# An encoder block on one Trainium2 core: the second use of a weight tile loads the split parts that the first use stored

## The chip, the core and the metric

The kernel runs on one core of a Trainium2 chip. The core has a matrix engine (TensorE, PE in the profile), a vector engine (VectorE, DVE), a scalar engine (ScalarE, ACT), a general engine (GpSimd, POOL) and a queue engine (SyncE, SP), from which this kernel issues its DMA transfers. 16 DMA engines move data between the chip's memory and the on-chip buffers. The metric is the device time of one execution in microseconds.

## What is computed

One layer of an encoder, batch 1, 2048 tokens, width 1024, everything in float32:

```python
h  = rmsnorm(x, norm1_g)
P  = h @ w_in          # columns: attention q | k | v | SSD z | SSD x,B,C | SSD dt
yB = windowed_attention(q, k, v, sink, cos, sin)    # |i-j| <= 128, partial rotary
yA = ssd_mixer(z, xbc, dt, ...)                     # conv(5), SiLU, two chunked scans, gated norm
x  = x + concat(rmsnorm(yB), yA) @ w_out
x  = x + conv_glu_ffn(rmsnorm(x))                   # w_up, conv(3), gate, w_down
return rmsnorm(x, final_norm_g)
```

The change concerns the product `h @ w_in` alone, and of `w_in` the 1664 columns that come out with channels on the partitions: 13 tiles of 128 channels, `w_ch`, each 128 x 1024 floats (512 KB). The remaining columns (`w_t`) come out with tokens on the partitions and have loads of their own.

## The kernel before

**Three products for one.** PE multiplies in a rounded 32-bit format (fp32r). To keep float32's precision, each operand is split into a rounded high part and a low part that holds what the rounding left. `mm3` issues three matmuls for each product: high by high, high by low, low by high (L106, L107, L108). A weight tile therefore has to exist as two tiles, `whi` and `wlo`.

**The weight path.** All weight tiles stand in one list, `wplan`, in the order of their use, and `next_w` hands them out. `w_raw` loads a raw tile into the buffer tag `wraw` (L127). `w_split` casts it on ACT into `whi` (L141) and subtracts on DVE or POOL into `wlo` (L142):

```python
A.copy(hi[:, :m], raw[:, :m])
(V if i < WV or i in WVS else G).tensor_tensor(lo[:, :m], raw[:, :m], hi[:, :m].bitcast(F32), ALU.subtract)
```

The tables `WV` and `WVS` say by number in the list which tiles DVE subtracts. Each of the three tags has two buffers. `next_w` splits tiles i and i+1 and loads i+1 and i+2, so a tile is split while PE works on the one before it; its `whi` buffer comes free when PE is done with the tile two places before.

**Two halves.** The tokens are taken in two halves of 1024, each as two banks of 512. So each `w_ch` tile is used twice, and loaded and split twice (tiles 11 and 12 in the second half twice: once for each of its banks). A string for each half (`PLAN`) sets the order of the source: `F` is the pair of tiles 0 and 1, `C5` a tile of the convolved SSD input, `R10` a rotary tile of the attention, `t11` token-major tiles, letters steps of scan and attention. In the first half the list's numbers 0 to 12 are the tiles 0, 1, 5, 7, 4, 3, 2, 11, 10, 12, 6, 9, 8. In the second half numbers 13 to 25 are 0, 1, 2, 5, 4, 3, 6, 7, 10, 9, 8, 11, 12; numbers 26 to 37 are pieces of `w_out`, and 38 and 39 are tiles 11 and 12 again. From 40 on come `w_up`, `w_down` and the rest of `w_out`. Below, "tile 15" means number 15 of this list.

**What sets the order.** The kernel is written as a sequence of tile operations; a scheduler with a timeline simulation then fixes the order of instructions on every engine, ahead of the run. Every DMA of the kernel goes through SP's queue, in that order: a transfer that waits for a buffer holds up what stands behind it. Among these are the x tiles of the first normalisation (L244), the transposed x (L273), the rotary tables `cs` (L425; 512 KB each), the copies of the rotated rows (L433, L434), and the stores and loads of the scan and the attention.

**Consumers of the tables.** A rotary tile multiplies its table with the row factors on DVE (L428), then the PE result with the table (L436); the other terms run on POOL (L446, L447). L436 also reads the PSUM bank that PE then reuses.

Of the kernel before, what the change touches and what calls it, by code (L numbers as in the profile page):

```python
# [10 lines left out]
F32 = mybir.dt.float32  # L11
F32R = mybir.dt.float32r
# [5 lines left out]
P = 128  # L18
# [39 lines left out]
def block_kernel(ctx: ExitStack, tc: tile.TileContext, a: dict, out: bass.AP):  # L58
    nc = tc.nc
# [3 lines left out]
    wpool = ctx.enter_context(tc.tile_pool(name="wpool", bufs=2))  # L63
# [26 lines left out]
    def dram(name, shape):  # L90
        return dpool.tile(shape, F32, tag=name, name=name)
# [9 lines left out]
    s_d = dram("s_d", [6, P, 512])  # L101
    acs_d = dram("acs_d", [NC * H, 2, P])
    mix_d = dram("mix_d", [4, P, TB])

    def mm3(ps, whi, wlo, xhi, xlo, first, last):
        nc.tensor.matmul(ps, whi, xhi, start=first, stop=False)  # L106
        nc.tensor.matmul(ps, whi, xlo, start=False, stop=False)  # L107
        nc.tensor.matmul(ps, wlo, xhi, start=False, stop=last)  # L108
# [6 lines left out]
    wplan = [(a["w_ch"][c], 1024) for c in range(2)]  # L115
    wraws, wdone, wplace = {}, {}, {}
    wpos = [0]

    def w_raw(i):
        if i >= len(wplan) or i in wraws:  # L120
            return
        src, m = wplan[i]
        raw = wpool.tile([P, 1024], F32, tag="wraw", name="wraw")
        dst = raw[:, :m]
        if len(src.shape) == 3:
            dst = dst.rearrange("p (i n) -> p i n", i=2)
        nc.sync.dma_start(dst, src)  # L127
        wraws[i] = raw

    def w_split(i):  # L130
        if i >= len(wplan) or i in wdone:
            return
        w_raw(i)
        m = wplan[i][1]
        raw = wraws[i]
        if i in wplace:
            hi, lo = wplace.pop(i)
        else:
            hi = wpool.tile([P, 1024], F32R, tag="whi", name="whi")
            lo = wpool.tile([P, 1024], F32R, tag="wlo", name="wlo")  # L140
        A.copy(hi[:, :m], raw[:, :m])  # L141
        (V if i < WV or i in WVS else G).tensor_tensor(lo[:, :m], raw[:, :m], hi[:, :m].bitcast(F32), ALU.subtract)  # L142
        wdone[i] = (hi, lo)

    def next_w():
        i = wpos[0]
        wpos[0] += 1
        w_split(i)
        w_raw(i + 1)
        w_split(i + 1)  # L150
        w_raw(i + 2)
        return wdone.pop(i)
# [1048 lines left out]
    def wo_pair(cp, s):  # L1201
        src = a["w_out"][2 * cp : 2 * cp + 2, :, 512 * s : 512 * s + 512]
        return src.rearrange("c p n -> p c n"), 1024

    for half in range(2):
        for tok in PLAN[half].split():
            if tok == "F":
                wplan += [(a["w_ch"][c], 1024) for c in range(2 * half)]
            elif tok == "P3":
                wplan += [(a["w_ch"][c], 1024) for c in (11, 12)]  # L1210
            elif tok[0] in "HQ":
                wplan.append(wo_pair(int(tok[1]), "HQ".index(tok[0])))
            elif tok[0] in "CR":
                wplan.append((a["w_ch"][int(tok[1:])], 1024))
    wplan += [wo_pair(cp, 1) for cp in range(4)]
    wplan += [(a["w_ch"][c], 1024) for c in (11, 12)]
    for j in range(NB):
        for g, (k0, nk) in enumerate(GROUPS):
            wplan += [(a["w_up"][k0 + i, q], 1024) for i in range(nk) for q in range(2)]
# [146 lines left out]
    for j in range(NB):  # L1366
# [4 lines left out]
        for g, (k0, nk) in enumerate(GROUPS):  # L1371
# [3 lines left out]
            i = 0  # L1375
            if j == 0 and g == 0 and UP2:
# [9 lines left out]
                i = 2  # L1386
# [91 lines left out]
def build(arrays):  # L1478
    import concourse.bacc as bacc

    nc = bacc.Bacc("TRN2", target_bir_lowering=False, num_devices=1)
    aps = {
        n: nc.dram_tensor(f"in_{n}", v.shape, mybir.dt.from_np(v.dtype), kind="ExternalInput").ap()
        for n, v in arrays.items()
    }
    out = nc.dram_tensor("out_0", (D, S), F32, kind="ExternalOutput").ap()
    with tile.TileContext(nc, schedule_with_timeline_sim=True) as tc:
        block_kernel(tc, aps, out)
    return nc
# [9 lines left out]
```

## Time and profile before

| | before |
|---|---|
| median of 3 runs | 2496.29 us (2495.41 to 2500.74) |
| profiled execution | 2505.61 us |
| its span | 2503.8 us |
| PE busy | 2373.5 us, 95% |
| DVE, ACT, POOL busy | 70%, 43%, 45% |
| granted TensorE clock, mean | 0.975 of full speed |
| DMA | 332.13 MB, mean 133 GB/s |

A time in a row is counted from the start of the span of the profiled execution. In a window's row each engine has its busy time and its number of instructions; PEclk is the granted TensorE clock as a share of full speed, DMA the busy share of the 16 DMA engines. In a timeline row the bracket at the end holds the idle time just before the instruction and what ended it. In a row of waits stand the engine, its operation and line, what it waited for, then the total, the number of waits and the longest one.

### The profile page before, as it was taken

To read this page: it belongs to the slowest core of one execution; us is meant where nothing else is said; L and a number is where in the kernel's file an instruction comes from. 1 tells how busy PE (TensorE), PEld (TensorE's weight loads), DVE (VectorE), ACT (ScalarE), POOL (GpSimd) and SP (SyncE) were. 2 spreads that over 40 slices of the span, in tenths; PEclk is the share of its full clock that TensorE was granted. 3 is DMA by queue.
4 is the path that set the end of the run, shared out by engine and by line. 5 is a ranking of instruction groups with operands and counts; after the bars stand their busy time and mean duration, and the time that the engine had idled before them with its cause. 6 is when DMAs were issued, how large, how long until landed. Compare 5 with 4: busy or idle time off the path is not lost.

```text
span 2503.8 us, 31565 instructions
## 1 busy us (share of the span) xinstructions
PE 2373.5 (95%) x11440; PEld 1975.7 (79%) x11440; DVE 1761.6 (70%) x3116; ACT 1088.3 (43%) x1814; POOL 1126.9 (45%) x625
## 2 busy tenths in 40 slices
PE   8998999887899999999999999999999999999997
PEld 6877798766688887777788777777888877788887
DVE  5778778878786775468978685689686555844445
ACT  5444565444354444335444443254444433433334
POOL 1045314564545435445444443554444445544444
PEclk9999999998899999999999999999999999999998
DMA  6567445774433343333434333343443232332232
GB/s 225 178 198 224 126 147 186 247 246 149 141 116 122 127 140 97 101 112 122 126 131 137 99 133 114 90 129 119 129 127 96 84 114 89 118 101 93 93 94 84
DMA packets 176047, 332.13 MB, mean 133 GB/s; under 512 B 13202, under 2 KB 84242, under 8 KB 175892
## 3 DMA queue, kind: packets, MB, share of 16 engines
q1 hardware_dynamic: 175892, 330.12, 41.2%
q8 instruction: 90, 1.47, 0.2%
q14 instruction: 65, 0.53, 0.1%
HBM read 284.06 MB, written 44.71 MB: 131 GB/s over the span
## 4 chain that ended last, share of the span: by engine, by line
PE 50%; DVE 9%; POOL 2%; issue 2%; ACT 1%; DMA 1%; DVEq 0%; POOLq 0%; SPq 0%; ACTq 0%
PE up_b L108 9%; PE up_b L107 9%; PE up_b L106 9%; PE dn_b L106 3%; PE dn_b L107 3%; PE dn_b L108 3%; DVE fa L1047 2%; POOL wlo L142 2%; PE dn L107 2%; PE dn L106 2%; PE dn L108 2%; PE wo_b L108 2%; PE wo_b L106 2%; PE wo_b L107 2%; DVE m_lo L972 1%
## 5 line engine op out<-in xcount | busy, mean ns | idle before, releaser
L142 POOL TENSOR_TENSOR wlo<-wraw,whi 128x1024 fp32r<-128x1024 f32 (+1 forms) x306 | 739.0, 2416 | 901.8 <-ACT whi L141 849.8
L108 PE MATMUL up_b<-h_hi,wlo 128*128 128x512 f32 x1392 | 555.3, 399 | 15.9 <-POOL wlo L142 15.8
L107 PE MATMUL up_b<-h_lo,whi 128*128 128x512 f32 x1392 | 553.0, 398 | 4.7 <-DVE h_lo L208 4.7
L106 PE MATMUL up_b<-h_hi,whi 128*128 128x512 f32 x1392 | 554.3, 399 | 1.4 <-ACT whi L141 0.9
L141 ACT CAST whi<-wraw 128x1024 fp32r<-128x1024 f32 (+1 forms) x330 | 338.9, 1027 | 453.0 <-PE up_b L107 117.8
L1047 DVE SCALAR_TENSOR_TENSOR fa<-up_b,fcw,fa 128x511 f32<-128x511 f32 (+2 forms) x396 | 271.4, 686 | 206.1 <-ACT fa L1049 201.7
L108 PEld LDWEIGHTS up_b<-h_hi,wlo 128*128 128x128 f32 x1392 | 264.6, 190 | 79.8 <-POOL wlo L142 21.8
L107 PEld LDWEIGHTS up_b<-h_lo,whi 128*128 128x128 f32 x1392 | 264.3, 190 | 63.3 <-DVE h_lo L208 5.9
L106 PEld LDWEIGHTS up_b<-h_hi,whi 128*128 128x128 f32 x1392 | 264.1, 190 | 60.1 <-ACT whi L141 2.3
L106 PE MATMUL dn_b<-f,whi 128*128 128x512 f32 x528 | 211.4, 400 | 0.4 <-DVE x L1090 0.2
L107 PE MATMUL dn_b<-f,whi 128*128 128x512 f32 x528 | 208.8, 395 | 0.0
L108 PE MATMUL dn_b<-f,wlo 128*128 128x512 f32 x528 | 204.3, 397 | 0.0
L1069 ACT ACTIVATE fth<-fa 128x512 f32<-128x512 f32 (+1 forms) x88 | 55.6, 632 | 217.3 <-DVE fa L1047 165.3
L1074 ACT CAST f<-fth 128x512 fp32r<-128x512 f32 (+1 forms) x88 | 54.4, 620 | 207.6 <-DVE fth L1071 169.2
L1090 DVE TENSOR_TENSOR x<-x,dn_b 128x512 f32<-128x512 f32 x144 | 97.5, 680 | 61.0 <-PE dn_b L108 60.9
L1049 ACT ACTIVATE fa<-up_b,fcw 128x512 f32<-128x512 f32 x176 | 136.0, 774 | 0.2
L106 PEld LDWEIGHTS dn_b<-f,whi 128*128 128x128 f32 x528 | 99.7, 189 | 22.8 <-DVE x L1090 1.1
L108 PEld LDWEIGHTS dn_b<-f,wlo 128*128 128x128 f32 x528 | 99.3, 188 | 22.4 <-POOL wlo L142 0.3
L107 PEld LDWEIGHTS dn_b<-f,whi 128*128 128x128 f32 x528 | 99.2, 188 | 21.2
L875 DVE SCALAR_TENSOR_TENSOR ab<-ab,ldt,mask 128x128 f32<-128x128 f32 x256 | 106.7, 482 | 11.7 <-DMA ab<-acs_d 11.5
L1075 DVE TENSOR_TENSOR f<-fth,f 128x512 fp32r<-128x512 f32 (+1 forms) x88 | 79.2, 900 | 30.3 <-ACT f L1074 29.4
L106 PE MATMUL pj_b<-h_hi,whi 128*128 128x512 f32 x208 | 85.4, 411 | 12.3 <-ACT h_hi L235 7.1
(328 smaller groups left out, 5047.1 us busy)
## 6 DMA issues: line engine op xcount, KB each, us to landing
wraw<-in_w_up SPq DMA_DIRECT2D x176, 512.0 KB
wraw<-in_w_dn SPq DMA_DIRECT2D x64, 512.0 KB
wraw<-in_w_out SPq DMA_DIRECT2D x36, 512.0 KB
ab<-acs_d SPq DMA_DIRECT2D x32, 512.0 KB
wraw<-in_w_ch SPq DMA_DIRECT2D x28, 512.0 KB
wraw<-in_w_dn SPq DMA_DIRECT2D x32, 384.0 KB
ak<-ks_d SPq DMA_DIRECT2D x14, 768.0 KB
cs<-in_rope SPq DMA_DIRECT2D x20, 512.0 KB
```

Source lines behind the costliest of these rows:

```text
L106: nc.tensor.matmul(ps, whi, xhi, start=first, stop=False)
L107: nc.tensor.matmul(ps, whi, xlo, start=False, stop=False)
L108: nc.tensor.matmul(ps, wlo, xhi, start=False, stop=last)
L141: A.copy(hi[:, :m], raw[:, :m])
L142: (V if i < WV or i in WVS else G).tensor_tensor(lo[:, :m], raw[:, :m], hi[:, :m].bitcast(F32), ALU.subtract)
L875: (G if i < SUBP[0 if first else 1] else V).scalar_tensor_tensor(ab[:, i, d], ab[:, i, d], ldt[:, d, c, h : h + 1], mask3[:, 2 * d * P : ( ...
L1047: V.scalar_tensor_tensor(o, src, w(q), o, ALU.mult, ALU.add)
L1049: A.activation(ai[:, 0:TB], u, AF.Identity, bias=w(3), scale=w(2))
L1069: A.activation(th[:, :n], acc[:, 0, :n], AF.Tanh)
L1074: A.copy(fs[:, idx, 0, :n], th[:, :n])
L1075: V.tensor_tensor(fs[:, idx, 1, :n], th[:, :n], fs[:, idx, 0, :n].bitcast(F32), ALU.subtract)
L1090: V.tensor_tensor(xv, xv, ps[i], ALU.add)
```

## The change

In the first half, after a `w_ch` tile has been split, both parts are also stored to a new array `wch_d` in the chip's memory (L152 of the changed kernel). When the same tile comes up again, `w_split` takes two buffers and loads the two parts into them (L142 of the changed kernel); there is no raw load, no cast and no subtract. `w_ch` notes for each tile whether this is its first use. Thus 13 tiles make 26 stores of 512 KB; numbers 13 to 25, 38 and 39 make 30 loads of 512 KB, in place of 15 raw loads, 15 casts on ACT, and 15 subtracts (numbers 13, 14, 19, 21 and 25 on DVE, the other ten on POOL). The rest of the kernel is written as before.

```diff
+    wch_d = dram("wch_d", [13, 2, P, 1024])
+    wkeep, wch_at = {}, {}
...
+    def w_pair(i):
+        return [wpool.tile([P, 1024], F32R, tag=t, name=t) for t in ("whi", "wlo")]
+
     def w_raw(i):
-        if i >= len(wplan) or i in wraws:
+        if i >= len(wplan) or i in wraws or i in wsame:
             return
...
     def w_split(i):
         if i >= len(wplan) or i in wdone:
             return
+        if i in wsame:
+            wdone[i] = w_pair(i)
+            for t, src in zip(wdone[i], wsame[i]):
+                nc.sync.dma_start(t.bitcast(F32), src)
+            return
         w_raw(i)
...
         A.copy(hi[:, :m], raw[:, :m])
         (V if i < WV or i in WVS else G).tensor_tensor(lo[:, :m], raw[:, :m], hi[:, :m].bitcast(F32), ALU.subtract)
+        if i in wkeep:
+            for t, dst in zip((hi, lo), wkeep[i]):
+                nc.sync.dma_start(dst, t[:, :m].bitcast(F32))
         wdone[i] = (hi, lo)
...
+    def w_ch(c):
+        i = len(wplan)
+        dst = [wch_d[c, q] for q in range(2)]
+        if c in wch_at:
+            wsame[i] = dst
+        else:
+            wch_at[c] = i
+            wkeep[i] = dst
+        wplan.append((a["w_ch"][c], 1024))
```

The scheduler's order changes with it, in the input projection alone; three places follow. In the names below the number at the end only tells one buffer's use from another's. The first place is SP's queue near the start: `xt0` is an x tile, `wraw` the raw loads of tiles 2 and 3, `cs11` a rotary table, `xb3` transposed x. Before:

```order
L244 DMA xt0_170<-in_x 128x1024
L127 DMA wraw_231<-in_w_ch 128x1024
L127 DMA wraw_237<-in_w_ch 128x1024
L425 DMA cs11_512_1073<-in_rope 128x2x512
L273 DMA xb3_0_1552<-in_xT 128x512
```

Now:

```order
L254 DMA xt0_171<-in_x 128x1024
L152 DMA wch_d_109<-whi_224 128x1024
L152 DMA wch_d_109<-wlo_225 128x1024
L152 DMA wch_d_109<-whi_230 128x1024
L152 DMA wch_d_109<-wlo_231 128x1024
L133 DMA wraw_236<-in_w_ch 128x1024
L133 DMA wraw_244<-in_w_ch 128x1024
```

The four stores of tiles 0 and 1 have come between the x tile and the raw loads; the x tiles 1 to 3 stand some rows behind, in both.

The second place is SP's queue near the end of the first half, at the last rotary tile: `cs8` are its two tables, `rw` the copies of rotated rows, `qs_d` stored queries, `ct0` an operand of the scan. Before:

```order
L434 DMA rw8_512_1728<-rw8_512_1728 8x512
L454 DMA qs_d_103<-rw9_512_1638 128x2x512
L425 DMA cs8_512_1725<-in_rope 128x2x512
L433 DMA rw8_512_1728<-rw8_512_1728 8x512
L434 DMA rw8_512_1728<-rw8_512_1728 8x512
L454 DMA qs_d_103<-rw9_0_1650 128x2x512
L425 DMA cs8_0_1743<-in_rope 128x2x512
```

Now:

```order
L443 DMA rw8_512_1751<-rw8_512_1751 8x512
L444 DMA rw8_512_1751<-rw8_512_1751 8x512
L142 DMA whi_2144<-wch_d_109 128x1024
L142 DMA wlo_2145<-wch_d_109 128x1024
L435 DMA cs8_0_1766<-in_rope 128x2x512
L856 DMA ct0_4010<-ct_d0_94 128x2x128
L685 DMA pb_d_105<-stateb_3458 128x512
L464 DMA qs_d_103<-rw9_512_1663 128x2x512
L435 DMA cs8_512_1748<-in_rope 128x2x512
```

The two loads of tile 14 (`whi_2144`, `wlo_2145`) now stand ahead of both tables; its raw load stood farther up, before the copies of the rotated rows.

The third place is PE at the passage from the pair of tiles 13 and 14 (`pj0_1`, `pj1_1`, worked on in turn) to tile 15 (`pj2_1`) in the second half; `sc` are score products of the attention. Before, the last products of tile 13 are these, and after them 18 matmuls of `pj1_1` and four `sc` stand ahead of the first of tile 15:

```order
L108 MATMUL pj1_1_b0_2119<-h2_True_hi_2074,wlo_2122 128x512
L107 MATMUL pj0_1_b0_2117<-h2_True_lo_2075,whi_1671 128x512
L108 MATMUL pj0_1_b0_2117<-h2_True_hi_2074,wlo_1672 128x512
L106 MATMUL pj1_1_b0_2119<-h2_True_hi_2074,whi_2121 128x512
L107 MATMUL pj1_1_b0_2119<-h2_True_lo_2075,whi_2121 128x512
```

Now:

```order
L109 MATMUL pj0_1_b0_2140<-h2_True_lo_2098,whi_1696 128x512
L110 MATMUL pj0_1_b0_2140<-h2_True_hi_2097,wlo_1697 128x512
L110 MATMUL pj1_1_b0_2142<-h2_True_hi_2097,wlo_2145 128x512
L108 MATMUL pj1_1_b0_2142<-h2_True_hi_2097,whi_2144 128x512
L109 MATMUL pj1_1_b0_2142<-h2_True_lo_2098,whi_2144 128x512
L110 MATMUL pj1_1_b0_2142<-h2_True_hi_2097,wlo_2145 128x512
```

Tile 13's last two products have moved eight rows toward tile 15, so that ten matmuls of `pj1_1` and the four `sc` are left between.

## Rows read from the trace of the kernel before

**Rows 1.** The page: busy time of the engines; shares of the chain by engine.

```profile
PE 2373.5 (95%) x11440; PEld 1975.7 (79%) x11440; DVE 1761.6 (70%) x3116; ACT 1088.3 (43%) x1814; POOL 1126.9 (45%) x625
...
PE 50%; DVE 9%; POOL 2%; issue 2%; ACT 1%; DMA 1%; DVEq 0%; POOLq 0%; SPq 0%; ACTq 0%
```

**Rows 2.** PE's waits in 420 to 640: us in total, times, longest.

```profile
PE mt L936 <- ACT y L933: 6.4, 2, 4.5
PE pt L763 <- DVE mxs L737: 5.9, 1, 5.9
...
PE wh_b L107 <- DVE m_lo L972: 4.9, 5, 2.7
...
PE pq_b L108 <- POOL wlo L142: 0.5, 1, 0.5
```

**Rows 3.** Windows: length, PE, PEld, DVE, ACT, POOL, PEclk, DMA share, GB/s.

```profile
0.00:660.00 660.00, 587.59 (x2961) 500.20 (x2962) 505.48 (x809) 330.53 (x603) 261.85 (x188) 0.95 0.59 190
...
350.00:400.00 50.00, 50.00 (x290) 44.96 (x289) 35.98 (x94) 26.46 (x51) 9.83 (x7) 1.00 0.39 122
...
420.00:640.00 220.00, 182.91 (x942) 156.30 (x941) 181.65 (x316) 97.78 (x200) 120.87 (x93) 0.91 0.65 209
```

**Rows 4.** Groups of 0 to 660: count, busy us, mean ns, idle before and releasers.

```profile
L142 POOL TENSOR_TENSOR wlo<-wraw,whi 128x1024 fp32r<-128x1024 f32 x18 | 46.1, 2560 | 88.6 <-ACT whi L141 64.1 <-DVE x L997 12.4 <-DVE rsm L751 12.2
...
L141 ACT CAST whi<-wraw 128x1024 fp32r<-128x1024 f32 x42 | 43.9, 1045 | 44.9 <-PE pj_b L107 25.8 <-PE pq_b L107 7.1 <-DMA wraw<-in_w_out 4.0
...
L142 DVE TENSOR_TENSOR wlo<-wraw,whi 128x1024 fp32r<-128x1024 f32 x24 | 32.6, 1357 | 22.3 <-ACT whi L141 22.3
```

**Rows 5.** A window near the start, columns as in rows 3.

```profile
24.00:26.00 2.00, 2.00 (x10) 1.63 (x9) 0.40 (x2) 1.82 (x4) 0.00 (x0) 1.00 1.05 396
```

**Rows 6.** Timeline near the start, SP, ACT, DVE, PE: start, us, instruction.

```profile
1.20 0.42 SPq L127 DMA_DIRECT2D wraw<-in_w_ch  x1
...
22.37 1.58 SPq L127 DMA_DIRECT2D wraw<-in_w_ch  x2
27.74 2.40 SPq L244 DMA_DIRECT2D xt<-in_x  x3
...
5.13 1.04 ACT L141 CAST whi<-wraw 128x1024 fp32r<-128x1024 f32 x1 [3.11 <-DMA wraw<-in_w_ch]
...
30.48 1.04 ACT L141 CAST whi<-wraw 128x1024 fp32r<-128x1024 f32 x1
...
31.55 1.23 DVE L142 TENSOR_TENSOR wlo<-wraw,whi 128x1024 fp32r<-128x1024 f32 x1 [5.12 <-ACT whi L141]
...
34.70 0.40 PE L106 MATMUL pj_b<-h_hi,whi 128*128 128x512 f32 x1
```

**Rows 7.** Timeline and windows at the end of the rotary section, 210 to 228.

```profile
211.19 2.16 POOL L447 TENSOR_TENSOR cs<-cs,rw 128x512 f32<-128x512 f32 x1
...
212.11 2.31 DVE L428 TENSOR_TENSOR cs<-cs,rx_half 128x1024 f32<-128x1024 f32 x1
...
225.35 1.22 DVE L428 TENSOR_TENSOR cs<-cs,rx_half 128x1024 f32<-128x1024 f32 x1 [3.21 <-DMA cs<-in_rope]
...
227.35 0.64 PE L500 MATMUL tp_b<-thi,h_hi 128*128 128x328 f32 x1 [6.36 <-DVE cs L436]
...
210.00:215.00 5.00, 5.00 (x30) 4.51 (x29) 5.00 (x4) 1.28 (x3) 3.76 (x3) 1.00 0.38 128
...
224.00:227.30 3.30, 0.00 (x0) 0.00 (x0) 1.92 (x3) 0.00 (x0) 0.65 (x1) 0.50 1.04 330
...
227.40:230.60 3.20, 3.20 (x12) 3.20 (x13) 2.64 (x3) 1.61 (x4) 1.80 (x2) 0.50 0.77 234
```

**Rows 8.** Timeline at the passage to tile 15, ACT and PE.

```profile
275.37 1.05 ACT L141 CAST whi<-wraw 128x1024 fp32r<-128x1024 f32 x1 [4.98 <-PE pj_b L107]
...
280.04 0.40 PE L106 MATMUL pj_b<-h_True_hi,whi 128*128 128x512 f32 x1
```

**Rows 9.** Timeline of subtracts after 400 us, POOL and DVE.

```profile
405.23 2.44 POOL L142 TENSOR_TENSOR wlo<-wraw,whi 128x1024 fp32r<-128x1024 f32 x1 [4.68 <-ACT whi L141]
...
633.99 2.40 POOL L142 TENSOR_TENSOR wlo<-wraw,whi 128x1024 fp32r<-128x1024 f32 x1 [2.14 <-ACT whi L141]
...
518.49 2.25 DVE L142 TENSOR_TENSOR wlo<-wraw,whi 128x1024 fp32r<-128x1024 f32 x1 [0.77 <-ACT whi L141]
```

More of the change, by code (lines that the diff above doesn't have):

```diff
@@ L117, in block_kernel @@
     wpos = [0]
+    wsame = {}
+    def w_pair(i):
+        return [wpool.tile([P, 1024], F32R, tag=t, name=t) for t in ("whi", "wlo")]
     def w_raw(i):
-        if i >= len(wplan) or i in wraws:
+        if i >= len(wplan) or i in wraws or i in wsame:
             return
@@ L135, in w_split @@
         raw = wraws[i]
[L136 to L140, printed above, removed]
+        hi, lo = wplace.pop(i) if i in wplace else w_pair(i)
         A.copy(hi[:, :m], raw[:, :m])
         (V if i < WV or i in WVS else G).tensor_tensor(lo[:, :m], raw[:, :m], hi[:, :m].bitcast(F32), ALU.subtract)
+        if i in wkeep:
+            for t, dst in zip((hi, lo), wkeep[i]):
+                nc.sync.dma_start(dst, t[:, :m].bitcast(F32))
         wdone[i] = (hi, lo)
@@ L1203, in wo_pair @@
         return src.rearrange("c p n -> p c n"), 1024
+    def w_ch(c):
[7 more added lines that the diff above has]
+        wplan.append((a["w_ch"][c], 1024))
+    for c in range(2):
+        wch_at[c] = c
+        wkeep[c] = [wch_d[c, q] for q in range(2)]
     for half in range(2):
@@ L1207, in block_kernel @@
             if tok == "F":
-                wplan += [(a["w_ch"][c], 1024) for c in range(2 * half)]
+                for c in range(2 * half):
+                    w_ch(c)
             elif tok == "P3":
-                wplan += [(a["w_ch"][c], 1024) for c in (11, 12)]
+                w_ch(11)
+                w_ch(12)
             elif tok[0] in "HQ":
@@ L1213, in block_kernel @@
             elif tok[0] in "CR":
-                wplan.append((a["w_ch"][int(tok[1:])], 1024))
+                w_ch(int(tok[1:]))
     wplan += [wo_pair(cp, 1) for cp in range(4)]
-    wplan += [(a["w_ch"][c], 1024) for c in (11, 12)]
+    for c in (11, 12):
+        w_ch(c)
     for j in range(NB):
```

## The prediction

> **What bounds the kernel now.** I read the page first. TensorE (PE) is busy 95% of the span, and the page's chain that ended last is half PE and 9% VectorE (DVE) [rows 1]. Those shares add up to some 65% of the span: the chain leaves part of it uncovered, and it names mostly lines of the feed-forward part, which the change does not touch. What the change touches lies in the input projection, the first 660 us, so I read that stretch from windows and waits.
>
> The second thing to see is that PE is nearly always busy there too: 587.6 of 660 us, with 72 us idle, of which 37 us lie in 420 to 640 [rows 3]. So everything that the change could give back is bounded by those idle times, and by the clock that falls after some of them. [...]
>
> Third, who is waited for? In the list of PE's waits in 420 to 640 a split part of a weight tile costs PE 0.5 us at most, once, for one from POOL. At the top stand results of DVE, with one of ACT: 5.9 us for a row maximum of the attention, 4.9 us for the low part of the mixed rows, 6.4 for ACT's scaled y of the scan [rows 2]. Weight splitting is done early enough; PE waits for DVE's other work. So the splits that go can help only by giving DVE time.
>
> The DMA columns come fourth. DMA is busy 0.59 of the first 660 us, at 190 GB/s, and 0.65 in 420 to 640 [rows 3]. Into this part the change puts 26 stores and 30 loads of 512 KB in place of 15 raw loads: 41 more transfers, 21.5 MB.
>
> **The change part by part.** The profiled execution took 2505.6 us (span 2503.8) and the median of the three runs is 2496.3. All terms below are differences inside the profiled one; I add them to the median.
>
> *What goes.* Fifteen splits: a cast each on ScalarE (ACT, 1.05 us), a subtract each, ten of them on POOL (2.56 us), five on DVE (1.36 us) [rows 4]: 15.7 us of ACT, 25.6 of POOL, 6.8 of DVE. ACT is busy half of the stretch (330 of 660) and POOL 40% [rows 3]; PE waits for neither's splits, so their own time is worth nothing. What counts is DVE: its 6.8 us, and the time that POOL's subtract holds it up. For the latter there is a pair of rows: the rotary product of L428 took 1.22 us at 225.35 and 2.31 us at 212.11, where a two-input POOL operation ran from 211.19 to 213.35 [rows 7]. That is 1.09 us for each meeting.
>
> [...]
>
> Where does this fall? From 350 to 400 PE is busy 50.0 of 50 us [rows 3] and nothing can be won there. Only what lies after 400 can shorten an idle time: five of the ten POOL subtracts, from 405.23 to 633.99, and one of the five on DVE, of 2.25 us [rows 9]: 5 x 1.09 + 2.25 = 7.7 us of DVE. In the best case all of it comes off PE's idle time, and two falls of the clock go with it: a fall lasts at least the 3.3 us that rows 7 show, at half speed 1.7 us lost, 3.4 for two. So the ends are 0 and -11. I take **-3**: DVE is busy 182 of the 220 us in 420 to 640 [rows 3], not always, and its shares of PE's waits come from single late results, so less than half of what is freed will stand in the right place.
>
> *The stores at the start.* The order of the SP queue (first piece of the change's section) puts the four stores of tiles 0 and 1 ahead of the raw loads of tiles 2 and 3, which went out at 22.37 behind one x load, and of the three x loads of 27.74 [rows 6]. DMA is full there: share 1.05, 396 GB/s [rows 5]. Four stores are 2.10 MB, 5.3 us at that rate. Tile 2's low part was finished at 31.55 + 1.23 = 32.8, its high part at 31.5, and PE's first matmul of tile 2 started at 34.70 [rows 6]. Later by 5.3 us, high comes at 36.8 and low at 38.1: PE stands 2.1 to 3.4 us. But the raw tile may have lain there before its cast began at 30.48, since that cast shows no wait [rows 6]: a load into an empty queue took from 1.20 to 5.13, 3.9 us [rows 6], so it may have landed as early as 26.3, and the stall would be nothing. Above, a fall of the clock (1.7) could follow a 3.4 us stall. Ends 0 and +5, taken **+2**.
>
> [...]
>
> *The other 22 stores of the first half.* 11.5 MB, 29 us of DMA at 396 GB/s, spread over 40 to 215 us. Most fall beside idle DMA and cost nothing. The place where they could cost is the rotary section, where SP also fetches the tables (cs) that DVE waits for. The worst wait there is at 225.35: DVE had waited 3.21 us for a table, and PE 6.36 us for what DVE made of it, while DMA ran at 1.04 [rows 7]. In the new order two loads of tile 14 stand ahead of a table load. They are 1.05 MB, 2.6 us; before them, in 210 to 215, DMA was busy only 0.38 [rows 7], so they may also be through in time. Ends 0 and +2.6 for this place; other tables are the slower rival's matter. I take **+2.6**, since DMA is full where the table travels.
>
> *The loads at the start of the second half.* Tile 15's parts need the buffers of tile 13, and so wait for PE to finish it, as the cast did: that cast began at 275.37 after waiting 4.98 us for PE, and PE began tile 15 at 280.04 [rows 8], with 18 matmuls and 4 score products between. In the new order only 10 and 4 stand there (third piece). 4.67 us x 14/22 = 3.0 us of cover for a load that took 3.9 alone [rows 6]: **+0.9**, ends 0 (loads wait less than that) and +3.6, when the two parts come one behind the other at 1.3 us each and the four next loads compete. For the other tiles SP waits where ACT waited, for the same matmul, with a whole tile's 48 matmuls as cover (8.3 us at the 290 in 50 us of [rows 3]) against two loads of 3.9: nothing. While SP stands in such a wait, what is queued behind it stands too (state, query and key loads of the scan and the attention); these are used a tile later, and I cost them at nothing, +3 if that cover is gone.
>
> *Moved work.* The scheduler reorders matmuls, DVE and ACT work in the whole stretch; nothing in the trace prices it. Its bounds are the terms above: +-4.
>
> Sum: -3 + 2 + 2.6 + 0.9 = **+2.5**, 2496.3 + 2.5 = 2498.8 us. A measurement of this kernel can tell about 0.2% (5 us) from no change, so this is no change.
>
> **The rivals.**
> *Slower: the tables queue behind the stores.* The change makes SP's single queue carry pairs of 512 KB between the rotary tables. If one pair stands ahead of each table that DVE already waits for (five such waits in 660 us, the one in rows 7 among the longest), DVE loses 5 x 2.6 = 13 us and, as it is the engine PE waits for there, half of it reaches PE: 6.5. With the start (+2) and tile 15 (+0.9) and no relief: +9.4, **2505.7 us**. It decides as soon as the pairs reach DMA within 3 us ahead of a table. For it: DMA at 0.94 to 1.04 around 225, the order. Against: 210 to 215 with 0.38, and whatever pairs are issued long before a table.
> *Faster: DVE gets its time back.* If the meetings with POOL are what makes DVE late after 400, the whole -11 comes, and the tables travel unhindered: -11 + 2 + 0.9 = -8.1, **2488.2 us**. For it: DVE tops PE's waits [rows 2], and one clear meeting [rows 7]. Against: eight of POOL's 18 subtracts, those of the output projection, stay [rows 4], some of them in the same stretch.
> *It does not do what it says.* If the parts came too late always, PE would show waits for loads on each of the 15 tiles; the order has most of them a tile ahead, so I give this no time of its own, inside the slower one.
>
> **How the numbers follow.** Forecast, within 0.2% (2491.3 to 2501.3): 0.45. Slower by over 0.2%: 0.33, from the table rival, the reordering's bad end and a long stall at the start. Faster by over 0.2%: 0.22. The forecast time is the likeliest case's. The range reaches to both rivals, from 2488 to 2508: below it lies reordering on top of full relief (0.1), above it the table rival with the start's upper end (0.1).
>
> **What would show it.** Start: a PE gap before tile 2 of about 2 us with the first wait on the cast or the subtract, near 35 us. Rotary section: the wait of 6.36 us near 227 grows to about 9, with the table as DVE's releaser. Half two: PE's first matmul of tile 15 waits about 1 us on a load; no other tile's load appears among PE's longer waits. Relief: idle time of PE in 420 to 640 falls from 37 to about 34 us, and DVE's mean for two-input operations falls there. After 675 us nothing differs. I am wrong if PE's idle time in 420 to 640 changes by more than 8 us either way, if a load of the second half holds SP so long that scan or attention work waits behind it, or if the whole stretch is shorter because the new order itself fills the gaps.

## The result: slower, by an order that the scheduler chose

| | before | changed |
|---|---|---|
| median | 2495.85 us (2494.27 to 2500.74, 4 runs) | 2510.02 us (2508.23 to 2510.57, 4 runs) |
| profiled execution | 2505.61 us | 2509.82 us |
| ratio | | 1.0052, 95% interval 1.0035 to 1.0070 |

The change costs 13 us (9 to 17), by the ratio times 2496 us, as all differences below. The forecast was 2498.8 us, and the range ended at 2508.

The profiled execution of before that the prediction read was some 10 us longer than its median. So the kernel before was profiled again (e1 below), and the changed one is set beside that one too. The changed kernel, the page (busy time; DMA in all; chain by engine):

```profile
PE 2375.8 (95%) x11440; PEld 1973.7 (79%) x11440; DVE 1741.1 (69%) x3111; ACT 1074.9 (43%) x1799; POOL 1094.2 (44%) x615
...
DMA packets 181951, 353.63 MB, mean 141 GB/s; under 512 B 13858, under 2 KB 84898, under 8 KB 181796
...
PE 47%; DVE 11%; POOL 2%; issue 2%; ACT 2%; DMA 1%; DVEq 0%; POOLq 0%; ACTq 0%
```

Against [rows 1] DVE, ACT and POOL are busy 20, 13 and 33 us less, and 21.5 MB more are moved (332.13 MB before). What was meant to happen did happen. The engine that sets the pace, PE, is as busy as it was, and the kernel is longer.

Windows of the changed kernel, columns as in [rows 3]:

```profile
24.00:26.00 2.00, 2.00 (x10) 1.65 (x9) 0.67 (x4) 1.83 (x6) 0.02 (x1) 1.00 1.04 414
25.00:50.00 25.00, 21.78 (x97) 17.01 (x96) 7.97 (x13) 11.82 (x20) 2.03 (x2) 0.99 0.95 378
420.00:640.00 220.00, 176.96 (x900) 151.28 (x898) 172.93 (x312) 92.41 (x194) 109.44 (x91) 0.88 0.66 218
```

From 420 to 640 PE's idle time is 43 us where [rows 3] had 37 (e1: 38), and the granted clock 0.88 where it was 0.91 (e1: 0.92): the relief that was expected there is a loss. The list of PE's waits in 420 to 660 of the changed kernel says on what:

```profile
PE mt L946 <- ACT y L943: 7.8, 2, 6.9
PE cb L895 <- DVE am L790: 5.3, 1, 5.3
PE pt L773 <- DVE mxs L747: 5.3, 1, 5.3
PE wh_b L108 <- DVE cs L446: 4.9, 1, 4.9
PE sc L745 <- DMA ak<-ks_d: 4.4, 1, 4.4
...
PE pq_b L108 <- DMA whi<-wch_d: 1.7, 1, 1.7
...
PE pq_b L110 <- DMA wlo<-wch_d: 0.8, 1, 0.8
```

Two of these rows are loads of stored parts, 2.5 us together. The others are waits on work that the change does not touch: rotary results (`cs`), sums of the scan and the attention, a load of keys (`ak`). Some of them ([rows 2]: `mt`, `pt`) were there before, some are new. By itself that list does not say why; the experiments do.

### The profile page after: what moved, and what is told of

It is laid out like the page before. It is cut to its first block, busy times and chain, and to the rows that moved or that the text cites. A ratio compares the mean times of both kernels' runs of the same rounds, so it can differ in the third digit from the quotient of the medians.

```text
span 2507.7 us, 31610 instructions
## 1 busy us (share of the span) xinstructions
PE 2375.8 (95%) x11440; PEld 1973.7 (79%) x11440; DVE 1741.1 (69%) x3111; ACT 1074.9 (43%) x1799; POOL 1094.2 (44%) x615
## 4 chain that ended last, share of the span: by engine, by line
PE 47%; DVE 11%; POOL 2%; issue 2%; ACT 2%; DMA 1%; DVEq 0%; POOLq 0%; ACTq 0%
PE up_b L110 8%; PE up_b L109 8%; PE up_b L108 8%; PE dn_b L108 3%; PE dn_b L109 3%; PE dn_b L110 3%; DVE fa L1057 3%; PE dn L109 2%; PE dn L108 2%; PE dn L110 2%; PE wo_b L110 2%; PE wo_b L108 2%; PE wo_b L109 2%; POOL wlo L149 1%; DVE m_lo L982 1%
## 5 line engine op out<-in xcount | busy, mean ns | idle before, releaser
L149 POOL TENSOR_TENSOR wlo<-wraw,whi 128x1024 fp32r<-128x1024 f32 (+1 forms) x296 | 713.4, 2411 | 860.3 <-ACT whi L148 834.7
L148 ACT CAST whi<-wraw 128x1024 fp32r<-128x1024 f32 (+1 forms) x315 | 323.3, 1026 | 434.7 <-PE up_b L109 115.3
```

## The experiments

**e1: the kernel before, a second look.**

> The kernel before, unchanged, for a second profiled execution. The one shown took 2505.6 us, about 10 us more than the kernel's median (2495.9). If that execution was an odd one, this one takes about 2496 and its span about 2494, and the first matmul of the feed-forward part (647.0 us in the profile shown) comes some us earlier, so that the 6.5 to 7.5 us by which it is later in the changed kernel (654.5) grows toward the 14 us between the medians. If the profiler itself costs 10 us, this one takes 2505 again, and 7 us of the 14 have still to be found behind 655 us.

Measured: 2495.4 us, span 2493.6. The first execution was an odd one, and the profiler does not cost 10 us. Start of the feed-forward part (PE timeline: start, us), in e1:

```profile
644.47 0.73 PE L106 MATMUL up_b<-h_hi,whi 128*128 128x512 f32 x2 [0.18 <-ACT h_hi L207]
```

and in the changed kernel:

```profile
654.49 0.48 PE L108 MATMUL up_b<-h_hi,whi 128*128 128x512 f32 x1
```

10.0 us of the difference stand there, at the end of the projection: 4.8 us are more idle time of PE up to that point (71.7 us against 66.9), 5.2 us more busy time for the same work, at a mean granted clock of 0.95 against 0.96. Behind it PE's order still differs up to some 720 us, and from there it is the same. The two spans differ by another 4.1 us behind that matmul; since the two executions of the kernel before differ there by 7.7 us, this tells nothing.

**e2, e3, e4: the parts of the change, each left to the scheduler.** e2 has the stores alone; e3 has the loads alone, and they all read the parts of one stored tile, so that its second half multiplies with that tile's weights throughout; e4 is the change without numbers 38 and 39:

```diff
 # e2
         if c in wch_at:
-            wsame[i] = dst
+            pass
 # e3
-            wsame[i] = dst
+            wsame[i] = [wch_d[4, q] for q in range(2)]
...
-            wkeep[i] = dst
+            if c == 4:
+                wkeep[i] = dst
...
-        wkeep[c] = [wch_d[c, q] for q in range(2)]
 # e4
-    for c in (11, 12):
-        w_ch(c)
+    wplan += [(a["w_ch"][c], 1024) for c in (11, 12)]
```

> The first half's 26 stores stay; the second half loads raw tiles and splits them as before. If the traffic of the stores is the cause, this costs 8 us or more of the 14 (2504 to 2510). If the second half's loads are the cause, because SP stands waiting for PE to give up a buffer and holds what is queued behind, this costs 0 to 4 (2496 to 2500). If the cause is only that the scheduler's order has changed, nothing orders the runs: this can come out anywhere between -5 and +14.

> Only one tile's two parts are stored (its second-use copy stands for all), and all 30 loads of the second half read them: 24 of the 26 stores are left out, the loads stay. The second half's projection so multiplies with one tile's weights throughout. If the loads and the held queue are the cause, this costs 8 to 14 us (2504 to 2510). If the stores are, it costs 0 or gives some back (2490 to 2498). By the theory of the changed order alone, no forecast: -5 to +14.

> As the changed kernel, but numbers 38 and 39 (tiles 11 and 12 for the last bank) are loaded raw and split as before. In the changed kernel PE waits 2.5 us there for the two parts, and the copies of the rotated rows are issued at 648.8 us instead of 638.7. If that passage costs, 3 to 5 us come back (2505 to 2507). If the loss lies in 400 to 620 us, the time stays within 2 us of the changed kernel's (2508 to 2512).

| | median us | ratio to before | 95% interval |
|---|---|---|---|
| e2 stores only | 2512.8 | 1.0062 | 1.0045 to 1.0078 |
| e3 loads only | 2486.3 | 0.9958 | 0.9944 to 0.9971 |
| e4 38 and 39 split | 2505.5 | 1.0037 | 1.0023 to 1.0052 |

e4 gives back 3.7 us, as expected if that passage costs, but its interval overlaps the changed kernel's, and its order there is one of its own. The loads, the suspect after the list above, gain 10 us, and the stores cost 15: that reads like traffic. But e2 and e3 add to +5, not +13. And e2's second half holds no instruction that the kernel before does not hold; its order does differ there, in 705 PE rows through the whole projection.

**e5, e6: stores without the order, the order without stores.** Which stores move the second half's order was looked for in the order alone. It turns on number 11. e5 stores all but number 11, and from about 205 us on every engine has the order of before. e6 stores only numbers 10 and 11, and from there on has e2's order but for 14 PE rows. Both load and split in the second half as e2 does.

```diff
 # e5
-        if i in wkeep:
+        if i in wkeep and i != 11:
 # e6
-        if i in wkeep:
+        if i in wkeep and i in (10, 11):
...
 # e5, e6
         if c in wch_at:
-            wsame[i] = dst
+            pass
```

> Stores only, as in e2, but for number 11 (tile R9), which isn't stored: 24 of the 26 stores remain. With that the scheduler's order of every engine is the one of the kernel before from about 205 us on (row 844 of PE on; in the first half 74 PE rows differ), where e2's differs in 705 rows to the end of the projection. If the stores' traffic makes e2 slow (+15 us), this costs about 24/26 of it, +13 to +15 (2509 to 2512). If the order that the scheduler chose for the second half makes it slow, nothing is left: -1 to +3 (2495 to 2500).

> Stores only, and of the 26 only four: those of numbers 10 and 11. From about 205 us on the order of every engine is that of e2 but for 14 PE rows. By traffic this costs 4/26 of e2's 15 us, 0 to +3 (2496 to 2500). By the order it costs what e2 costs: +11 to +16 (2507 to 2513).

Measured: e5 2497.1 us, ratio 1.0000 (0.9986 to 1.0013); e6 2512.8 us, 1.0056 (1.0038 to 1.0074). 24 stores cost nothing, to some 3.5 us either way; four stores cost as much as 26. So the traffic of all the stores is not the cause. What these two runs leave are the order and the two stores of number 11 themselves; e9 and e10 below part them. A place where e6's order loses can be read. e6, PE and DVE timeline and windows (columns as in [rows 3]) near 345 us:

```profile
342.44 0.16 DVE L805 TENSOR_SCALAR arc<-aps 128x1 f32<-128x1 f32 x1 [0.71 <-PE aps L803]
344.33 0.17 DVE L761 TENSOR_TENSOR rsm<-rsm,es 128x4 f32<-128x4 f32 x1 [1.74 <-ACT es L760]
344.41 0.68 DVE L810 TENSOR_TENSOR am<-am,apr 128x512 f32<-128x512 f32 x1
...
345.28 1.23 DVE L376 SCALAR_TENSOR_TENSOR cacc<-cu,cacc 128x1024 f32<-128x1024 f32 x1
...
346.81 0.17 DVE L549 SCALAR_TENSOR_TENSOR dtraw<-tp_b,vecs 128x16 f32<-128x16 f32 x1
...
347.03 0.53 PE L510 MATMUL tp_b<-thi,h_True_hi 128*128 128x328 f32 x1 [3.42 <-DVE dtraw L549]
...
347.00:350.40 3.40, 3.37 (x13) 3.37 (x14) 1.65 (x4) 2.81 (x6) 2.27 (x1) 0.53 1.01 339
```

e5, the same work:

```profile
335.68 0.17 DVE L549 SCALAR_TENSOR_TENSOR dtraw<-tp_b,vecs 128x16 f32<-128x16 f32 x1
...
336.15 0.15 DVE L805 TENSOR_SCALAR arc<-aps 128x1 f32<-128x1 f32 x1
336.22 0.16 DVE L549 SCALAR_TENSOR_TENSOR dtraw<-tp_b,vecs 128x16 f32<-128x16 f32 x1
337.27 0.16 DVE L761 TENSOR_TENSOR rsm<-rsm,es 128x4 f32<-128x4 f32 x1 [0.89 <-ACT es L760]
...
337.28 0.31 PE L510 MATMUL tp_b<-thi,h_True_hi 128*128 128x328 f32 x1
```

`dtraw` empties the PSUM bank that PE's next `tp_b` needs; what it reads was long there (PE's last `tp_b` before it started at 328.04). In the order of before DVE empties both banks, with one `arc` between, and attends to the attention's small sums (`rsm`, `am`) after; PE's first `tp_b`, at 337.28, shows no wait. In e6 `arc`, `rsm` and `am` stand ahead, and two of them have to wait for another engine: DVE idles 0.71 and 1.74 us with `dtraw` in the queue behind. PE then waits 3.42 us, and over the next 3.4 us its mean granted clock is 0.53: from 347.36 to 350.10 its `tp_b` matmuls start 0.27 us apart, from 350.63 on those of the same shape 0.15 us apart. e2 has the same wait in the same place (3.90 us at 346.0). Such waits recur: PE's list of e6 for 225 to 640 holds, among others,

```profile
PE sc L745 <- DVE mxs L747: 6.4, 3, 5.1
...
PE aps L803 <- ACT rw L451: 4.6, 1, 4.6
...
PE tp_b L510 <- DVE dtraw L549: 3.4, 1, 3.4
...
PE pj_b L108 <- DVE thi L541: 2.1, 1, 2.1
```

none of which stands among e5's. The first feed-forward matmul starts at 658.23 in e6 and at 640.17 in e5 (whose profiled execution, 2489.3 us, was 8 us under its median).

**e7, e8: the change for fewer tiles, left to the scheduler.** e7 stores and reloads numbers 0 to 10, e8 all but number 11.

```diff
 # e7
-        if c in wch_at:
+        if c in wch_at and wch_at[c] < 11:
...
+                if i < 11:
+                    wkeep[i] = dst
 # e8
-        if c in wch_at:
+        if c in wch_at and wch_at[c] != 11:
...
+                if i != 11:
+                    wkeep[i] = dst
```

> The whole change for numbers 0 to 10: 22 stores, and the second uses of those tiles (13 to 22 but for R9 and R8, 24, 25, 38, 39) are loads; tiles R9 and R8 are not stored and are split again. The order is a fourth one, near e3's up to about 300 us and unlike it after. If stores cost nothing and loads give back what e3 shows whatever the order, this takes 2484 to 2490. If the order decides, it lies anywhere from 2484 to 2512. If the stores' traffic costs, it is 2500 to 2508.

> The whole change but for number 11 (tile R9): not stored, and split again in the second half. 24 stores, 28 loads; the order is the changed kernel's but for 361 PE rows. If the loads give back 11 us whatever the order and stores cost nothing, 2484 to 2490. If the order decides, anywhere from 2484 to 2512, and different from e7. If traffic costs, 2500 to 2510, near the changed kernel.

Measured: e7 2501.9 us, 1.0014 (1.0002 to 1.0026); e8 2501.9 us, 1.0021 (1.0009 to 1.0033). Neither is at the 2484 to 2490 that loads with a fixed gain would give. They do not settle it: each has an order of its own.

**e9 to e12: operations and order crossed.** To hold the order still, a function chains each engine's instructions by edges that set the order and nothing else, by a table taken from another kernel's schedule. Left free are, in e9 and e11, the stores and the loads of stored parts, in e10 and e12 the raw loads, casts and subtracts of numbers 13 to 47; these stand where the scheduler puts them.

```diff
+def pin(tc):
+    info = mybir.DependencyInfo(mybir.DependencyClass.NoSync, mybir.DependencyReason.DATA)
...
+        for d in struct.unpack("<%dh" % (len(raw) // 2), raw):
+            at += d
+            ins = own[e][at]
+            if prev is not None:
+                tc.add_manual_dep(ins, prev.name, info, reason="pin")
+            prev = ins
...
         block_kernel(tc, aps, out)
+        pin(tc)
```

> The whole change, 26 stores and 30 loads, with the issue order of the kernel before: order-only edges chain each engine's instructions in the order of the kernel before, and only the stores and loads stand where the scheduler puts them. No PE row differs. This is the change at a fixed order, which my sum had priced. If the changed kernel's 14 us are the scheduler's order alone, it takes 2488 to 2498: the forecast's relief (-3, ends 0 and -11) with nothing for the stores, whose traffic e5 shows at 0. If the loads' waits on SP cost by themselves, 2502 to 2510.

> The kernel before, with its raw loads and splits and without a store, but every engine in the changed kernel's order (raw loads, casts and subtracts of numbers 13 to 47 stand free). If the order is the cause, it is as slow as the changed kernel or slower, since it has no relief: 2506 to 2516. If the stores and loads are the cause, 2494 to 2499.

> The whole change in the order of e3 (the loads alone), which took 2486. If stores cost nothing at a fixed order, this takes what e3 takes, 2483 to 2490, and is a version that beats both kernels. If the traffic of the other 24 stores costs something in the first half under this order, 2490 to 2500.

> The kernel before, with its raw loads and splits, in the order of e3. It tells e3's 11 us apart: if they came from the order, 2484 to 2490 again; if from the splits that are gone, 2494 to 2500, as the kernel before.

Median us, ratio to before and its interval:

| order | operations of before | operations of the change |
|---|---|---|
| of before | 2495.9 | e9 2500.4, 1.0014 (1.0001 to 1.0026) |
| of the change | e10 2519.7, 1.0088 (1.0067 to 1.0110) | 2510.0, 1.0052 (1.0035 to 1.0070) |
| of e3 | e12 2505.5, 1.0031 (1.0018 to 1.0044) | e11 2493.0, 0.9982 (0.9969 to 0.9996) |

Down a column the operations are the same and the order differs: 22 us for the kernel before, up to 17 for the changed one. Along a row the order is the same: +3.5 us in the order of before, -9 and -12 in the orders that the scheduler made for loads. That an order costs as much as e10 shows means also that e3's 10 us are not "what loads give": they are loads in an order made for them, while splits in that order lose 8. A part of e12's price is how its free splits fit in: from 420 to 660 us PE waits 9.1 us there for split parts of the output projection. In e10 it waits 0.3 us for them, though what the splits cost DVE and ACT is in its time too.

One result does not fit. e11 is e3's order with 24 more stores, and if stores cost nothing at a fixed order it was expected at 2483 to 2490. It came out 6.0 us above e3 (0.9982 against 0.9958), with intervals that just touch, where its expectation put the traffic. The two profiled executions differ by only 1.2 us at the first feed-forward matmul (638.1 and 639.3). So stores that cost nothing are shown for the order of before (e5, and e15 below), not for that of e3.

e10 has none of the change's stores and loads. Two waits of the changed kernel that neither e1 nor e9 has stand in e10's list for 420 to 660 again:

```profile
PE sc L770 <- DMA ak<-ks_d: 5.1, 1, 5.1
PE wh_b L136 <- DVE cs L471: 5.0, 1, 5.0
```

The first of them can be read. SP's issue of that load of keys and PE's first product with it, in the changed kernel:

```profile
567.08 0.46 SPq L712 DMA_DIRECT2D ak<-ks_d  x1
...
573.26 0.69 PE L745 MATMUL sc<-ak,aq 128*128 128x384 f32 x1 [4.38 <-DMA ak<-ks_d]
```

and in e1:

```profile
560.59 0.42 SPq L702 DMA_DIRECT2D ak<-ks_d  x1
...
582.41 0.33 PE L735 MATMUL sc<-ak,aq 128*128 128x384 f32 x1
```

The order of before leaves 21.8 us between the two, that of the change 6.2: the product has moved forward and the load back. No load of a stored part stands near (the last one before it was issued at 520.82).

In e9 the change is at one order and still gives nothing. PE's waits of e9 in 420 to 640, PE's and SP's timeline, and a window:

```profile
PE pq_b L137 <- DMA whi<-wch_d: 9.1, 2, 5.8
...
510.35 0.61 SPq L171 DMA_DIRECT2D whi<-wch_d  x1
...
517.52 0.77 PE L137 MATMUL pq_b<-h_True_hi,whi 128*128 128x512 f32 x1 [5.83 <-DMA whi<-wch_d]
...
620.48 0.33 SPq L171 DMA_DIRECT2D whi<-wch_d  x1
...
626.66 0.77 PE L137 MATMUL pq_b<-h_True_hi,whi 128*128 128x512 f32 x1 [3.27 <-DMA whi<-wch_d]
...
511.60:517.40 5.80, 0.09 (x1) 0.00 (x0) 2.75 (x4) 4.32 (x7) 2.26 (x3) 0.95 1.03 395
517.50:521.00 3.50, 3.48 (x11) 2.99 (x12) 1.23 (x1) 1.07 (x2) 1.43 (x2) 0.50 0.84 306
```

At the pairs 24/25 and 38/39, tiles 11 and 12 for one bank each, PE stands 9.1 us for a stored part, at the first place with DMA full (1.03, 395 GB/s) and the clock at 0.50 after. From issue to use these loads took 7.2 and 6.2 us. PE has the same order in e1 and e9, so the same instruction can be set side by side: at the `pt` near 600 us e9 is 5.1 us ahead (596.99 against 602.09), at the first feed-forward matmul, behind the second late load, 1.0 us late (645.46 against 644.47).

**e13, e14, e15: the late loads, and the stores once more.** e13 is e9 with numbers 25, 38 and 39 loaded raw and split as before; e14 does the same to e11; e15 is e3's program in the order of before, so e9 without 24 stores.

```diff
 # e13, e14
         if c in wch_at:
-            wsame[i] = dst
+            if i not in (25, 38, 39):
+                wsame[i] = dst
```

> The whole change in the order of the kernel before, as e9 (2500.4), but numbers 25, 38 and 39 are loaded raw and split as before: 24 loads are left. In e9 PE waits 5.8 us at 517.5 and 3.3 at 626.7 for a stored part that was issued only when PE gave its buffer up. If those late loads are what makes e9 no faster than the kernel before, some 9 us come back: 2489 to 2493. If the traffic or the held queue costs elsewhere, it stays at 2497 to 2501.

> The whole change in the order of e3, as e11 (2493.0), with numbers 25, 38 and 39 split as before. In e11 PE waits only 2.0 us for a late load (at 623.8), so little comes back here, and three casts and subtracts return to ACT, DVE and POOL: 2489 to 2495. Were the late loads worth as much as in e9 whatever the order, it would be 2484 to 2487.

> The loads alone (two stores, the second half multiplies with one tile's weights throughout, as in e3), but in the order of the kernel before. Against e9 it lacks 24 stores and nothing else. If stores are free at a fixed order, it takes e9's 2498 to 2502. If the stores are what keeps e9 from being faster, 2490 to 2495.

| | median us | ratio to before | 95% interval |
|---|---|---|---|
| e13 | 2494.8 | 0.9987 | 0.9977 to 0.9997 |
| e14 | 2494.3 | 0.9986 | 0.9976 to 0.9996 |
| e15 | 2498.3 | 1.0009 | 0.9997 to 1.0020 |

PE's waits of e13 in 420 to 640:

```profile
PE mt L975 <- ACT y L972: 6.6, 2, 4.5
PE pt L802 <- DVE mxs L776: 6.0, 1, 6.0
...
PE wh_b L138 <- DVE m_lo L1011: 4.4, 5, 2.2
...
PE pq_b L139 <- POOL wlo L178: 0.5, 1, 0.5
```

The row of 9.1 us is gone, and the list is that of the kernel before again ([rows 2]). 6.7 of the expected 9 us came back (to 4 us either way), from 1.0014 to 0.9987. In e3's order, where the late load was 2.0 us, nothing came back. e15 lies 1.2 us under e9 (1.0009 against 1.0014), with intervals that overlap: the stores cost little or nothing here too.

e11, e13 and e14 lie below both kernels, 3.2 to 4.5 us below the one before, with intervals that end just below 1.

## Why the prediction was wrong

**Moved work, "+-4", was the step that failed.** It was bounded by the other terms, which is no bound: no row stood behind it. With the change's operations, the new order costs 9.5 us (13.0 - 3.5, the change against e9; by the two intervals 4 to 15), with those of before 22 (e10, which includes the fit of the splits). Stores set such an order off (e6, four of them) without costing anything measurable themselves at the order of before (e5; e13, which has all 26). I had seen the moved rows in the order and shown three places of them, and took the rest for neutral on average. It need not be: the order of before was a good one among those seen here. Of seven orders that the scheduler made for variants left to it (e2, e3, e4, e6, e7, e8 and the change) one was faster than before; e5, whose order is that of before in all but the first 205 us, was as fast. The sign that was set for being wrong, over 8 us of idle time in 420 to 640, did not catch it: the idle time grew by 6 us, and half of the 10.0 us up to the feed-forward part is busy time at a lower granted clock (0.95 against 0.96).

**The loads of "the other tiles", "nothing".** I covered each with a whole tile's 48 matmuls and took 3.9 us for a load. Numbers 24, 25, 38 and 39 have one bank, half the matmuls; the loads took 6 to 7 us from issue to use; and with no raw buffer between, a load cannot go out until the buffer of the tile two places before is free (SP stood up to 11.6 us for one in 230 to 420 of the changed kernel). At the order of before that is 9.1 us of waits and 6.7 us of time (e9 against e13). In the changed kernel's own order PE waits 1.7 and 0.8 us there. For the whole tiles "nothing" held: SP stood 35.7 us in 230 to 420 for PE to give up buffers, but from 250 to 400 PE was busy 147.5 of 150 us.

**The start, "+2".** PE, ACT and DVE of the changed kernel near tile 2, and the raw loads on SP:

```profile
25.45 1.80 SPq L133 DMA_DIRECT2D wraw<-in_w_ch  x2
...
32.67 0.59 ACT L195 COPY rx_half<-rx_pr 128x512 f32<-128x512 f32 x1 [3.85 <-PE rx_pr L193]
33.15 1.05 ACT L148 CAST whi<-wraw 128x1024 fp32r<-128x1024 f32 x1
...
34.24 2.44 DVE L149 TENSOR_TENSOR wlo<-wraw,whi 128x1024 fp32r<-128x1024 f32 x2
...
34.26 0.50 PE L108 MATMUL pj_b<-h_hi,whi 128*128 128x512 f32 x1 [1.16 <-ACT whi L148]
```

The size was too large: the raw loads went out 3.1 us later than in [rows 6], the cast came 2.7 us later, and PE waited 1.16 us, but it had come there earlier, at 33.10 (34.26 - 1.16), and began tile 2 no later than the 34.70 of [rows 6]. No loss is left at this point. That the late raw load held the cast is not shown for this kernel: in its order a copy of row factors (`rx_half`) that waited 3.85 us for PE stands ahead of the cast, and the cast follows it at once. In e9, where the cast stands first, it began at 32.75 after 4.22 us of idle time whose end the profile does not name, and PE waited 1.04 us.

**The tables, "+2.6", and the slower rival.** DVE and PE of the changed kernel at the last rotary tile:

```profile
216.25 2.25 DVE L438 TENSOR_TENSOR cs<-cs,rx_half 128x1024 f32<-128x1024 f32 x1 [4.12 <-DMA cs<-in_rope]
...
227.28 1.23 DVE L438 TENSOR_TENSOR cs<-cs,rx_half 128x1024 f32<-128x1024 f32 x1 [3.50 <-DMA cs<-in_rope]
...
219.35 0.41 PE L510 MATMUL tp_b<-thi,h_hi 128*128 128x328 f32 x1 [2.48 <-DVE cs L446]
229.36 0.42 PE L510 MATMUL tp_b<-thi,h_hi 128*128 128x328 f32 x1 [3.74 <-DVE cs L446]
```

DVE does wait longer for tables (4.12 and 3.50 us, [rows 7] has 3.21), as the term said. PE's wait only splits: 2.48 + 3.74 = 6.2 us where there was one of 6.36. The rival had the right sign and the wrong mechanism: e5, with 24 stores among the tables, is as fast as before.

**Tile 15, "+0.9"**, was right in kind and half the size:

```profile
280.28 0.50 PE L108 MATMUL pj_b<-h_True_hi,whi 128*128 128x512 f32 x1 [0.43 <-DMA whi<-wch_d]
```

**The relief, "-3".** With the three late tiles left out, the change at the order of before gives -3.2 us (e13, -0.8 to -5.7), with 12 of the 15 splits gone. The size fits a fixed order; that it is the relief of DVE and POOL, and not something else that e13 also changes, was not tried by itself.

At a fixed order, then, the sum was +2.5 and the change costs +3.5 (e9, 0.2 to 6.5). That agreement is partly luck: the start and the tables were counted at 4.6 and gave nothing measurable, and the late loads, counted at nothing, gave 6.7. What the change does in the kernel as it stands is this plus the order, and the order was not forecast.

Open is which of the moved rows make up the order's price. Two places are read above: the `dtraw` of e2 and e6 (3.42 us, and a granted clock of 0.53 in the 3.4 us after), a wait that the changed kernel does not have, and the load of keys in the changed kernel and e10 (4.4 and 5.1 us). Neither was moved back by itself, and why the scheduler's simulation prefers such an order is not known.

## What to carry to other kernels

Where a scheduler with a model sets the order, an edit has two effects, what its instructions cost and what order it sets off, and the second can be larger than the first (9.5 us against 3.5 here); run the edit with the old order pinned before judging it, and try the scheduler's orders as a choice of their own. A DMA that writes straight into the operand's buffer gives up the raw buffer's prefetch, which cost PE 9.1 us of waits at the two shortest places (e9): check the cover tile by tile, at the shortest tile and with the time that a load takes where it stands (7.2 and 6.2 us from issue to use there, not the 3.9 us of the first load of [rows 6]). A small instruction that waits for another engine can cost what is queued behind it on its own engine (in e6, 0.71 and 1.74 us of idle DVE stood ahead of a wait of 3.42 us on PE).

## What was not expected of the hardware

The same operations in another order took 22 us more (e10). Stores and loads mixed ran at 414 GB/s over 2 us and at 378 over 25 us of the changed kernel, with DMA at 1.04 and 0.95, and 24 stores cost the kernel nothing that could be measured at the order of before (e5). PE's mean granted clock was 0.53 in the 3.4 us after a wait of 3.42 us (e6), and 0.50 in the 3.5 us after one of 5.83 (e9). By these clocks an estimated 1.6 us (0.47 x 3.4) and 1.8 us (0.50 x 3.5) come on top of the two waits.
